# A decoder step's mixer: its steps given other places beside the paged past

## The chip, the cores and the metric

One core of a Trainium2 chip runs the whole program. Its engines are TensorE (PE, matmul; PEld is its weight load), VectorE (DVE), ScalarE (ACT), GpSimd (POOL, which here mainly issues the gathers of cache pages) and SyncE (SP, which issues the other transfers). Each engine works through its own instructions in the order in which the program was built, and waits for others by semaphores. The metric is the device time of one execution in microseconds, as the median of several runs; lower is better.

## The reference

Two layers of a hybrid decoder, for 592 tokens: a prompt of 16 + 512 and 8 samples of 8 new tokens each. A layer is a half-step feed-forward block, a mixer and another half-step feed-forward block. Cut to the mixer:

```python
z, xbc, dt_raw, q, k, v = split(h @ w_in)
xbc_c = silu(causal_conv(xbc))                   # xs, B, C
y = ssd_scan(xs, softplus(dt_raw + dt_bias), -exp(A_log), B, C, h0) + D_skip * xs
y_ssd = group_rms_norm(y * silu(z)) * ssd_norm
q, k = rms_norm(q) * q_norm, rms_norm(k) * k_norm          # each head
# prompt: stick-breaking attention over itself, blocks of 128 queries
# samples: the same over 2048 cached keys in pages of 128, and their own new keys
#   z = q.k / 8 + bias;  w = sigmoid(z) * prod of (1 - sigmoid) over the later keys
o = w @ v
y_sb = rms_norm(o) * sb_out_norm
out = concat(y_ssd, y_sb) @ w_out
```

All is float32. A gemm keeps that precision by splitting each operand into a high and a low part and adding three products (high x high, low x high, high x low).

## The kernel before

Activations lie transposed: 8 tiles of 128 features x 592 tokens. `gemm` runs over pairs of output tiles of 128 columns; for each 512 rows of weights it loads `raw` (SP), splits it into `whi` (ACT, L595) and `wlo` (DVE, L596), and issues matmuls of 128x128 weights on 296 tokens into two PSUM banks (`g`, L605). When an output tile is complete, `done` takes it out of PSUM.

The mixer first runs the gemms of the queries (`queries`) and values (`values`), then traces the paged past (`past`), and after that the other steps in the order of the list `ORDER`. The past runs over 8 samples in 4 steps each: two page gathers of keys and two of values (POOL, L1508 and L1569), four transposes `kt` on DVE (L1519), a group of 32x128 matmuls `sc` for scores and `po` for weighing the values of the sample six steps behind, and per sample sigmoids, products `st` on DVE and transposes into weights. 34 such steps and four more for the last values.

The other steps: `dts` (time steps), `conv` (gemm of six tiles, convolution), `k` (gemm of the keys), `z` (gemm of the gates, `gate_in`, tiles `zi`, `zsg`), `scan` (six chunks of the state recurrence; the last, for the samples, also loads and stores their states), `kfin` (the keys' norm, `head_norm`: squares `hsq`, sums `ss`, a reciprocal root `ry`, spread over the partitions as `hb`, product onto `k`), `vout` (loads the values back as `vk`), `Pa-b` (prompt attention, blocks a to b-1 of 12, `pair_blocks`: scores `z`, sigmoids `be` and `st`, transposes `zt`, output `zo`), `mix` (gates and norm of the scan's output), `newk` (the samples' own keys), `tail` (the last 16 prompt queries), `kout` (stores keys), `xload` (loads the residual back). The output gemm `wo` comes last; its first half, over the scan's output, is tied behind the past's last scores, weights and weighing.

The order on each engine isn't written out. The program is built with a planner (`schedule_with_timeline_sim=True`) which, whenever an engine is free, takes the ready instruction with the lowest number. An instruction's number is its place in the traced program, unless `ahead` lowers it: `high_priority(now - d)` sets the number to d places after the past's first instruction. `PRI` gives d for a whole step, or, as `gemm:x`, for the weight splits and the `done` of a gemm; `UNIT` gives it for a single output tile of a gemm, a chunk of the scan or a prompt block. Where both are silent, a step keeps the number of its place, behind the whole past. The matmuls of a gemm always keep it.

Tiles come from pools with few slots: `g` has 3 PSUM banks (in the mixer behind the past `NARROW`, so all gemms, `kfin`, prompt blocks and `kout` draw on these three), `pm` 2, the others one each for the past; in SBUF `tmp` has 6 slots, `xh` 16 (the 16 tiles of the split hidden state until the last gemm of `w_in` has read them, then `vk`, `be`, `st` and the split operands of `wo`), and `kn` 6 for pages of keys and values alike.

```python
d = PRI.get(what) if what else PRI.get("gemm:" + self.gn, PRI["gemm"])
return nullcontext() if d is None else self.tc.high_priority(max(0, now - d))
```

Of the kernel before, what the change touches and what calls it, by code (L numbers as in the profile page):

```python
# [84 lines left out]
def pack(d):  # L85
# [6 lines left out]

ORDER = "dts conv k z scan kfin vout P0-8 P8-10 P10-12 mix newk tail kout xload".split()
PRI = {"gemm": 508, "scan": 0, "kfin": 1140, "newk": 2458, "dts": 0, "gemm:k": 0, "gemm:conv": 199, "gemm:wo": 693, "tail": 799, "gemm:z": 1391}
UNIT = {
    "conv0": 296, "conv2": 988, "conv3": 1825, "conv5": 1898, "k1": 434, "k2": 1127, "k3": 936, "prompt0": 1013,
    "prompt1": 2161, "prompt11": 2222, "prompt2": 2280, "prompt3": 1185, "prompt4": 2319, "prompt5": 1429,
    "prompt6": 106, "prompt7": 1403,  # L100
    "scan0": 467, "scan2": 75,
    "scan3": 879, "scan5": 123, "wo0": 0, "wo1": 2358, "wo2": 1775, "wo3": 86, "wo4": 1087, "wo5": 1599, "wo6": 529,
    "wo7": 1477, "z1": 0, "z2": 970, "z3": 1087,
}


class Kern:
# [515 lines left out]
    def ahead(self, what=None, unit=None):  # L623
# [3 lines left out]
        now = self.tc.cur_priority - self.p0  # L627
        u = UNIT.get(f"{what or self.gn}{unit}") if unit is not None else None
        if u is not None:
            return self.tc.high_priority(now - u)  # L630
        if what and unit is not None:
            return nullcontext()
        d = PRI.get(what) if what else PRI.get("gemm:" + self.gn, PRI["gemm"])
        return nullcontext() if d is None else self.tc.high_priority(max(0, now - d))
# [78 lines left out]
    def mixer(self, l):  # L713
# [36 lines left out]
        def xload():  # L750
            self.xtiles()
            for k in range(KD):
# [6 lines left out]
                 "tail": lambda: self.prompt_tail(q, S["k"]), "newk": lambda: self.new_keys(q, S["k"])}  # L759
        for st in ORDER:  # L760
            self.gn = st
# [885 lines left out]
```

## Time and profile before

| | us |
|---|---|
| median of 3 runs | 2688.8 |
| lowest, highest | 2679.9, 2701.8 |
| profiled execution | 2681.4 |
| its span, first to last instruction | 2679.6 |

The first mixer's work beside the past lies at about 527 to 920 us of the span, the second's at about 1864 to 2245; the feed-forward blocks around them keep PE busy without a break. In the span's strip of 40 slices these are slices 9 to 13 and 28 to 33. The profile gives busy time per engine for any stretch; on PE the matmuls are pipelined, so that busy time says when PE had work, not how well it was used. The granted clock is the share of full speed that PE was given. Rows by tile give the first and last start of each kind of instruction, and so when a step ran.

DVE is the second engine by load. The transfers of the past come at their highest rate in the later half of its time (slices 11 and 31 of the DMA strip):

```profile
DVE  6434346397886743444554343465878957444444
DMA  3232234467973222222222323244678731222222
GB/s 113 80 115 82 85 113 131 127 214 264 336 241 129 70 81 79 79 79 79 79 79 79 97 85 100 78 151 164 223 253 300 249 128 56 88 86 79 85 89 76
```

### The profile page before, as it was taken

What the parts mean: (1) busy time and instruction counts of PE and PEld (TensorE: products, weight loads), DVE (VectorE), ACT (ScalarE), POOL (GpSimd) and SP (SyncE); (2) the same over time, 40 slices, a digit from 0 to 9 for tenths busy, and PEclk for the clock granted to TensorE, in tenths of its full rate; (3) what the DMA queues carried; (4) which work ended last, traced back from release to release, by engine and by line L of the source; (5) the groups of instructions that cost most, each with busy time, mean ns of one, the idle gap of its engine ahead of it and who ended that gap; (6) DMA issues with size and microseconds to landing.
All of it is one profiled execution on the core that took longest, in us unless ns stands there. A gap on an engine that the chain in (4) does not pass through costs nothing.

```text
span 2679.6 us, 51326 instructions
## 1 busy us (share of the span) xinstructions
PE 2600.5 (97%) x21547; PEld 2466.6 (92%) x21547; DVE 1505.1 (56%) x3005; ACT 978.9 (37%) x1771; POOL 304.7 (11%) x288
## 2 busy tenths in 40 slices
PE   8999999999889999999999999999998899999999
PEld 7999999898657999999999999998886579999998
DVE  6434346397886743444554343465878957444444
ACT  3222224256564432222332222233566634223222
POOL 1000000034532100000000000001345411000000
PEclk9999999999989999999999999999998999999999
DMA  3232234467973222222222323244678731222222
GB/s 113 80 115 82 85 113 131 127 214 264 336 241 129 70 81 79 79 79 79 79 79 79 97 85 100 78 151 164 223 253 300 249 128 56 88 86 79 85 89 76
DMA packets 245112, 343.28 MB, mean 128 GB/s; under 512 B 32809, under 2 KB 196721, under 8 KB 244881
## 3 DMA queue, kind: packets, MB, share of 16 engines
q1 hardware_dynamic: 208016, 205.77, 24.7%
q0 software_dynamic: 36864, 134.23, 14.5%
q8 instruction: 169, 2.77, 0.4%
q14 instruction: 63, 0.51, 0.1%
HBM read 320.29 MB, written 19.66 MB: 127 GB/s over the span
## 4 chain that ended last, share of the span: by engine, by line
PE 84%; DVE 7%; issue 3%; ACT 3%; DMA 2%; POOL 1%; SPq 0%; DVEq 0%; POOLq 0%; ACTq 0%
PE g L605 72%; PE v L926 2%; DVE kt L1519 2%; PE po L211 1%; PE sc L211 1%; DMA v<-in_cache_v,vi 1%; DVE st L1298 1%; PE pw L476 1%; DMA kn<-in_cache_k,ki 1%; DVE pst L1298 1%; POOL v L1569 0%; PE z L208 0%; PE z L211 0%; DVE xl L447 0%; DVE wlo L596 0%
## 5 line engine op out<-in xcount | busy, mean ns | idle before, releaser
L605 PE MATMUL g<-xl,whi 128*128 128x296 f32 (+1 forms) x3392 | 1014.6, 299 | 2.7 <-DVE xl L447 2.7
L605 PE MATMUL g<-xh,wlo 128*128 128x296 f32 (+1 forms) x3392 | 1012.9, 299 | 2.0 <-DVE wlo L596 2.0
L605 PE MATMUL g<-xh,whi 128*128 128x296 f32 (+1 forms) x3392 | 1011.1, 299 | 1.5 <-DVE gs L231 1.2
L595 ACT ACTIVATE whi<-raw 128x512 fp32r<-128x512 f32 (+1 forms) x664 | 412.6, 622 | 1323.6 <-PE g L605 1240.5
L596 DVE TENSOR_TENSOR wlo<-raw,whi 128x512 fp32r<-128x512 f32 (+1 forms) x664 | 450.3, 678 | 582.8 <-ACT whi L595 529.7
L605 PEld LDWEIGHTS g<-xl,whi 128*128 128x128 f32 x3392 | 638.6, 188 | 5.6 <-DVE xl L447 3.6
L605 PEld LDWEIGHTS g<-xh,wlo 128*128 128x128 f32 x3392 | 638.7, 188 | 4.3 <-DVE wlo L596 2.5
L605 PEld LDWEIGHTS g<-xh,whi 128*128 128x128 f32 x3392 | 638.7, 188 | 4.0 <-DVE gs L231 1.4
L605 PE MATMUL g<-hl,whi 128*128 128x296 f32 (+1 forms) x1408 | 417.8, 297 | 0.0
L605 PE MATMUL g<-hh,wlo 128*128 128x296 f32 (+1 forms) x1408 | 417.6, 298 | 0.0
L605 PE MATMUL g<-hh,whi 128*128 128x296 f32 (+1 forms) x1408 | 416.7, 298 | 0.0
L1508 POOL DMA_INDIRECT kn<-in_cache_k,ki x128 | 128.3, 1003 | 1657.9 <-PE g L605 934.8
L605 PEld LDWEIGHTS g<-hl,whi 128*128 128x128 f32 x1408 | 265.2, 188 | 0.0
L605 PEld LDWEIGHTS g<-hh,wlo 128*128 128x128 f32 x1408 | 264.3, 188 | 0.0
L605 PEld LDWEIGHTS g<-hh,whi 128*128 128x128 f32 x1408 | 263.9, 188 | 0.0
L1519 DVE STREAM_TRANSPOSE kt<-kn 128x512 f32<-128x512 f32 x256 | 162.9, 681 | 27.7 <-PE sc L211 14.5
L704 DVE SCALAR_TENSOR_TENSOR x<-g,x 128x296 f32<-128x296 f32 (+1 forms) x192 | 88.1, 463 | 119.1 <-PE g L605 118.5
L1569 POOL DMA_INDIRECT v<-in_cache_v,vi x128 | 143.3, 1119 | 100.0 <-DVE kt L1519 36.1
L231 DVE TENSOR_TENSOR us<-g,R 128x296 f32<-128x296 f32 (+1 forms) x176 | 81.5, 464 | 129.1 <-PE g L605 129.0
L231 DVE TENSOR_TENSOR gs<-g,R 128x296 f32<-128x296 f32 (+1 forms) x176 | 80.6, 463 | 126.2 <-PE g L605 121.3
L691 ACT ACTIVATE hh<-us 128x592 fp32r<-128x592 f32 (+1 forms) x88 | 61.2, 696 | 64.3 <-DVE us L689 64.3
L605 PE MATMUL g<-mh,whi 128*128 128x296 f32 (+1 forms) x256 | 77.7, 312 | 2.4 <-ACT mh L1277 1.3
(372 smaller groups left out, 2838.8 us busy)
## 6 DMA issues: line engine op xcount, KB each, us to landing
raw<-in_ffn_w_gu SPq DMA_DIRECT2D x176, 512.0 KB
raw<-in_ffn_w_down SPq DMA_DIRECT2D x80, 512.0 KB
raw<-in_w_in SPq DMA_DIRECT2D x44, 512.0 KB
raw<-in_w_out SPq DMA_DIRECT2D x16, 512.0 KB
spill<-x SPq DMA_DIRECT2D x16, 296.0 KB
x<-spill SPq DMA_DIRECT2D x16, 296.0 KB
raw<-in_ffn_w_down SPq DMA_DIRECT2D x16, 256.0 KB
xt<-in_x_prompt SPq DMA_DIRECT2D x8, 256.0 KB
```

Of the source, the lines that this page charges most:

```text
L211: i = self.nc.tensor.matmul(*a, **k).ins
L231: self.nc.vector.tensor_tensor(tv[0:P, h, :], ps[h][0:P, 0:self.n], rv[0:P, h, :], ALU.mult)
L595: nc.scalar.activation(hi[:, 0:nk], s, AF.Copy)
L596: nc.vector.tensor_tensor(lo[:, 0:nk], s, hi[:, 0:nk].bitcast(F32), ALU.subtract)
L605: mm = nc.tensor.matmul(ps[h][:, 0:self.n], w[:, k, :], self.hv(x)[:, h, :], start=(first and k == 0 and i == 0), stop=(last and k == nk - ...
L691: nc.scalar.activation(hh[:, a:b], u[:, a:b], AF.Copy)
L704: nc.vector.scalar_tensor_tensor(v, p, 0.5, v, ALU.mult, ALU.add)
L926: nc.tensor.matmul(ps[c], x[:, t0:t0 + 128], w.rearrange("p x c -> p (x c)"), start=(k == 0 and i == 0), stop=(k == 7 and i == 2))
L1298: self.nc.vector.tensor_tensor_scan(sv, sv, self.zero[0:rows].to_broadcast([rows, b - a - 1]), 1.0, ALU.mult, ALU.add)
L1508: self.nc.gpsimd.indirect_dma_start(kn, None, self.kflat, bass.IndirectOffsetOnAxis(ap=self.kidx[self.l][:, s, 2 * i + u:2 * i + u + 1], a ...
L1519: self.nc.vector.transpose(kt[:, 2 * u:2 * u + 2].rearrange("p t h i -> p t (h i)"), kns[u][:, :, 256 * quad:256 * quad + 256])
L1569: self.nc.gpsimd.indirect_dma_start(v.rearrange("p k c -> p (k c)"), None, self.vflat, bass.IndirectOffsetOnAxis(ap=self.vidx[self.l][:, s ...
```

## The change

Only the three tables of places differ; no instruction is added or removed by them.

```diff
-ORDER = "dts conv k z scan kfin vout P0-8 P8-10 P10-12 mix newk tail kout xload".split()
-PRI = {"gemm": 508, "scan": 0, "kfin": 1140, "newk": 2458, "dts": 0, "gemm:k": 0, "gemm:conv": 199, "gemm:wo": 693, "tail": 799, "gemm:z": 1391}
-UNIT = {
-    "conv0": 296, "conv2": 988, "conv3": 1825, "conv5": 1898, "k1": 434, "k2": 1127, "k3": 936, "prompt0": 1013,
-    "prompt1": 2161, "prompt11": 2222, "prompt2": 2280, "prompt3": 1185, "prompt4": 2319, "prompt5": 1429,
-    "prompt6": 106, "prompt7": 1403,
-    "scan0": 467, "scan2": 75,
-    "scan3": 879, "scan5": 123, "wo0": 0, "wo1": 2358, "wo2": 1775, "wo3": 86, "wo4": 1087, "wo5": 1599, "wo6": 529,
-    "wo7": 1477, "z1": 0, "z2": 970, "z3": 1087,
-}
+ORDER = "dts conv k kfin z scan vout P0-12 mix newk tail kout xload".split()
+PRI = {"gemm": 508, "scan": 0, "kfin": 60, "newk": 560, "dts": 0, "gemm:k": 60, "gemm:conv": 0, "gemm:wo": 693, "tail": 600, "gemm:z": 120}
+UNIT = {f"prompt{i}": 300 + 25 * i for i in range(12)}
```

In the order of the trace, `kfin` stands between the gemms of keys and gates instead of behind gates and scan, and the twelve prompt blocks are traced in one run instead of three (a run finishes a block's output after the next block's scores are traced; at the end of a run it is finished at once). In the numbers, `kfin` goes from 1140 to 60, `newk` from 2458 to 560, `tail` from 799 to 600, the gates' splits and evictions from 1391 (single tiles 0, 970, 1087) to 120, the convolution's from 199 (single tiles up to 1898) to 0, the keys' from 0 (single tiles up to 1127) to 60. All chunks of the scan are at 0. Every prompt block has a number, 300 to 575 in steps of 25. The output gemm's eight tiles, which had numbers from 0 to 2358, are all at 693.

## The prediction

> **What bounds the kernel now.** I read the page first, for the engines' shares and the strip of 40 slices, then busy time in stretches of the first mixer and of the second, then the instructions on single tiles, to see which step ends each stretch.
>
> ```profile
> span 2679.6 us, 51326 instructions
> PE 2600.5 (97%) x21547; PEld 2466.6 (92%) x21547; DVE 1505.1 (56%) x3005; ACT 978.9 (37%) x1771; POOL 304.7 (11%) x288
> PE   8999999999889999999999999999998899999999
> PEclk9999999999989999999999999999998999999999
> ```
>
> PE works for 97% of the span, and every dip in its strip lies in the two mixers. Nothing in the change adds or removes arithmetic, so the time can change only by what PE idles there, and by the clock it gets. The two mixers, cut where the work changes (columns: length, busy us of PE, PEld, DVE, ACT, POOL, granted clock, DMA share, GB/s):
>
> ```profile
> 527.00:630.00 103.00, 101.04 (x1101) 91.73 (x1100) 85.64 (x203) 60.55 (x125) 34.71 (x32) 1.00 0.69 224
> 630.00:693.00 63.00, 60.83 (x750) 52.80 (x752) 53.35 (x118) 36.15 (x73) 30.58 (x30) 1.00 0.90 318
> 693.00:736.00 43.00, 35.71 (x497) 24.76 (x486) 37.01 (x89) 23.78 (x58) 23.23 (x24) 0.96 0.93 331
> 736.00:846.00 110.00, 93.26 (x1003) 67.34 (x1007) 91.25 (x213) 66.42 (x140) 36.13 (x33) 0.89 0.63 213
> 846.00:920.00 74.00, 72.17 (x581) 69.92 (x574) 51.08 (x92) 30.47 (x54) 10.13 (x6) 0.98 0.19 58
> 2036.00:2070.00 34.00, 28.65 (x416) 20.41 (x412) 27.74 (x59) 19.90 (x40) 18.07 (x16) 0.85 0.77 262
> 2070.00:2160.00 90.00, 74.19 (x854) 52.48 (x847) 80.80 (x183) 55.29 (x118) 40.77 (x36) 0.96 0.77 261
> ```
>
> While the gemms of conv, keys and gates last (527 to 693), PE is 97 to 98% busy: the gemms carry the largest numbers and fill every hole that the paged past leaves. From 693 no gemm is left until 846, and PE falls to 83% and 85%. Idle there: 43 - 35.71 = 7.3 and 110 - 93.26 = 16.7 us; in the second mixer 34 - 28.65 = 5.4 and 90 - 74.19 = 15.8. That is 45.2 us, 1.7% of the span, and it is nearly all that a new order can win. DVE is close behind: 91.25 of 110 and 80.80 of 90, 83% and 90%.
>
> What fills 693 to 736 is the norm of the keys (rows of the tile view: duration minimum/median/maximum, first and last start):
>
> ```profile
> L231 DVE TENSOR_TENSOR k<-g,R x8: 444/458/467, 593.4 to 628.0; 128x296 f32<-128x296 f32 x8
> L231 DVE TENSOR_TENSOR zi<-g,R x8: 444/454/466, 640.3 to 691.0; 128x296 f32<-128x296 f32 x8
> L879 ACT ACTIVATE hsq<-k x4: 678/680/682, 693.5 to 695.3; 128x592 f32<-128x592 f32 x4
> L890 DVE SCALAR_TENSOR_TENSOR k<-k,par,hb x8: 284/508/747, 721.1 to 735.7; 128x512 f32<-128x512 f32 x4, 128x80 f32<-128x80 f32 x4
> L947 SPq DMA_DIRECT2D vk<-vd x6: 338/536/600, 679.9 to 682.7; - x6
> L208 PE MATMUL z<-k,q x24: 376/587/792, 733.3 to 828.6; 64*128 64x512 f32 x8, 64*128 64x384 f32 x8, 64*128 64x256 f32 x8
> ```
>
> The raw keys are there at 628. Their squares wait until 693.5, although ACT is busy for only 36.15 of 63 us: `hsq` takes a slot of the pool `tmp` behind the gates' `zi`, whose last eviction is at 691. I read from this that slots go out in program order, so the order in `ORDER` decides. The norm then takes 42 us, and the first prompt scores follow at 733.3, 105 us after the keys. The values for them were asked for at 680.
>
> **The change, step by step.** Positions: `ahead` puts a step beside the past's own count, where only the first matmul of a `together` group counts. By my count one of the 8 sequences has 76 places (9 in each of its 4 steps for issues, transposes and the group, 8 sigmoids, 4 copies, 24 for the weights, 4 for the sum), so the past has 608 places and a step some 18. Before, all prompt numbers but one lie beyond 608 or are missing: blocks run where the past leaves room. After, they lie at 300 to 575, one per 25 / 18 = 1.4 steps.
>
> (a) `kfin` moves from behind the gates to behind the keys, and from 1140 to 60. It issues no DMA. On PE, ACT and DVE it now goes ahead of most of the past, and from the pools for PSUM banks (`g`, three) and `tmp` it takes its slots ahead of the gates' gemm. So the hole at 693 goes, 7.3 + 5.4 = 12.7 us. In its place comes a hole between keys and gates: `kfin` takes seven banks in turn, and the gates' gemm cannot have a pair until the last few are out. That gemm is what covers PE there; only past and scan remain. With the same chain at the same idle share this hole costs all 12.7 again. It should be shorter: the 13 operations of the reciprocal root run as follows,
>
> ```profile
> L523 DVE TENSOR_SCALAR ry<-rv x4: 141/172/180, 710.4 to 924.7; 128x5 int32<-128x5 int32 x2, 128x40 int32<-128x40 int32 x1, 128x10 int32<-128x10 int32 x1
> L529 DVE TENSOR_TENSOR rlo<-ry,rhi x5: 159/169/194, 501.8 to 928.6; 128x40 fp32r<-128x40 f32 x2, 128x5 fp32r<-128x5 f32 x2, 128x10 fp32r<-128x10 f32 x1
> ```
>
> each about 0.17 us long, 13 x 0.17 = 2.2 us of work, and yet from the keys' `ry` at 710.4 to the first `k` product at 721.1 there pass 11 us, since transposes of 0.68 us stand in front. With the front place I take half the chain and half the cost: 6.3 us. Net -6.3, ends -12.7 and 0.
>
> (b) The prompt blocks wait for `kfin` and for the slots of pool `xh` that the hidden state holds until the gates' gemm has read it. With 42 us of norm gone from behind that gemm and some 21 put in front of it, they begin about 20 us sooner. The past pays: blocks now stand ahead of its later steps on PE, ACT and DVE. How far it has come by then in the run before (DVE busy on the pages' transposes, 128 in all with 4 ahead of the first row):
>
> ```profile
> 520.00:693.00 173.00, 47.81 (x76) 1.00 0.76 258
> 693.00:736.00 43.00, 15.53 (x24) 0.96 0.93 331
> 736.00:846.00 110.00, 15.23 (x24) 0.89 0.63 213
> ```
>
> At 736 only 24 of 128 transposes are left, 6 steps; they and the value steps behind them share 110 us with 12 blocks. After, more steps share the stage with the same blocks. DVE is 83 and 90% busy here, so mixing them does not shrink the sum of DVE's work; I take 0 for the stage itself. Ends: half its idle goes, -16.3, or the past is late (the first rival).
>
> (c) `tail` from 799 to 600 and `newk` from 2458 to 560 come before the past's end. In the run before, `tail` stands in the output gemm, which is 97.5% busy in the first mixer (tile `z` and the scan operand `st`, first and second mixer):
>
> ```profile
> 846.00:920.00 74.00, 8.59 (x123) 6.63 (x114) 0.45 (x2) 4.67 (x12) 0.98 0.19 58
> 846.00:920.00 74.00, 3.91 (x4) 1.93 (x4) 0.98 0.19 58
> 2160.00:2245.00 85.00, 9.19 (x124) 6.87 (x122) 0.45 (x2) 4.67 (x12) 0.94 0.18 59
> 2160.00:2245.00 85.00, 4.48 (x6) 1.93 (x4) 0.94 0.18 59
> ```
>
> 8.59 + 9.19 = 17.8 us of PE move into a stage that idles; but 3.91 + 4.48 = 8.4 us of DVE go with them into a stage where DVE is 87% busy on average, which lengthens it by 8.4 / 0.87 = 9.7. Net -8.1, ends -17.8 and 0.
>
> (d) The whole scan at 0 (two chunks had 467 and 879), the conv evictions at 0, gates at 120, output gemm at 693. Until 693 PE is full, so moving DVE work about within this stretch frees nothing: 0. Its cover is the gemm filler; if DVE, 53.35 of 63 us busy, let it starve, a tenth of 63 us in each mixer would be 12.6 us. SP's and POOL's queues keep their transfers; only their order changes, and the past's pages queue behind evictions for at most a few operations.
>
> Sum: -6.3 + 0 - 8.1 + 0 = -14.4. The profiled execution took 2681.4 us (its span 2679.6 and 1.8 around it), so 2667.0. It is 7.5 us below the median of the three runs, 2688.8; against that median the forecast is 2674.4, say 2675, 0.5% less. A measurement of this kernel can tell about 1%, 27 us, from no change.
>
> **The rivals.** *The past is left over (slower).* Scan, norm, gates and most blocks now go first; what they take is taken from the past, which then ends alone, with no gemm to fill it, since the output gemm is tied behind the past's last scores. Price from 693 to 736: 24 transposes are 6 steps in 43 us at a DMA share of 0.93, 7.2 us a step, the best pace seen. PE's part of it in that stretch:
>
> ```profile
> 693.00:736.00 43.00, 5.47 (x160) 4.06 (x160) 15.53 (x24) 0.96 0.93 331
> 693.00:736.00 43.00, 7.44 (x99) 3.44 (x88) 0.59 (x2) 0.00 (x0) 0.96 0.93 331
> 693.00:736.00 43.00, 2.37 (x11) 1.54 (x11) 0.68 (x4) 1.20 (x2) 0.96 0.93 331
> ```
>
> (scores, weighing, weights): 15.3 / 6 = 2.5 us a step, so a step alone idles PE for 4.7 us. Five steps too many in each mixer cost 47 us: 2675 + 47 = 2722; six 56, 2731. It decides from (14.4 + 27) / (2 x 4.7) = 4.4 steps. For it: at 736 the past now has a lead of 104 transposes of 128, and it loses that lead. Against it: one block per 1.4 steps, the last at step 575 / 18 = 32 of 34, so by the numbers both end together.
>
> *The stage fills (faster).* If the hole in front of the gates closes (-12.7) and past and blocks together keep PE at the 96.6% of the stretch from 630 to 693, idle falls from 32.5 to 0.034 x 200 = 6.8, another -25.7: 2688.8 - 38.4 = 2650. Against it: that stretch had a gemm to fill it, this one has none, and DVE at 90% is in the way.
>
> *The clock comes back (faster).* In the four weak stretches PE's granted clock is 0.96, 0.89, 0.85 and 0.96; with PE full it is 1.00. Lost: 0.04 x 43 + 0.11 x 110 + 0.15 x 34 + 0.04 x 90 = 22.5 us. If denser work brought all of it back, 2675 - 22.5 = 2652. Against it: the stretch keeps most of its holes, and much of the small work waits on other engines, not on PE's clock. The Trainium skill, "TensorE: Matmul & The Clock Gate", Part 1, says that the array runs at half rate after an idle window of about 3.4 us and at full rate after a busy one; the rows above agree in direction, 1.00 with PE at 97% and 0.85 at 84%, and by that rule alone the sum would be the 2652 just worked out.
>
> *It does nothing.* If the gates' gemm loses in front what the blocks gain behind it, blocks start again at 733; with `tail` alone, -8.1, 2681.
>
> **How the numbers follow.** The forecast 0.45 and the change that does nothing 0.09 stay within 1% (2662 to 2716); the filled stage 0.14 and the clock 0.06 make 0.20 faster; the late past 0.26 is slower. The likeliest has its own range of 2662 to 2689. Range for all: from 2642, below both faster cases by what (c) has at its far end, to 2736, the late past with six steps in each mixer and a little of (d). Outside I leave half of the extremes, some 0.15 to 0.2.
>
> **What would show it.** Right: `hsq` follows the last raw key at once, and the norm takes some 20 us; the first prompt scores stand 15 to 25 us sooner after the mixer's start; `tail` lies before the past's last weighing; PE's idle in the four weak stretches, with the new holes between keys and gates, falls from 45 to about 31 us. (a) is wrong if the gates' gemm starts more than 35 us after the last key, (b) if the last block ends more than five steps before the past, (c) if the output gemm is no shorter. The whole is wrong if PE's idle in the mixers grows.

## The result: 0.5% slower

| | before | after |
|---|---|---|
| median, us | 2688.4 | 2700.4 |
| lowest, highest | 2679.9, 2701.8 | 2694.1, 2709.5 |
| profiled execution | 2681.4 | 2709.5 |

The ratio after to before is 1.0051, with a 95% interval of 1.0041 to 1.0062. The forecast was 0.5% less. Each median is over 20 executions. The two profiled ones stand at opposite ends of their runs, 7 us below the one median and 9 above the other, so a comparison of their stages shows the loss more than twice as large as the 12 us it is.

The page of the changed kernel (first the span and PE's total, then strips of 40 slices: busy share of PE and of DVE in tenths, the granted clock, the share of the DMA engines):

```profile
span 2707.5 us, 51317 instructions
PE 2619.9 (97%) x21547; PEld 2480.7 (92%) x21547; DVE 1504.2 (56%) x3005; ACT 984.5 (36%) x1775; POOL 313.3 (12%) x288
PE   8999999998978999999999999999989899999999
DVE  5444445397787744443554344464977967434444
PEclk9999999999988999999999999999989999999999
DMA  3232234467875122222222322244667941222222
```

PE's idle time is 2707.5 - 2619.9 = 87.6 us, where it was 79.1. In the two mixers alone it is 68.9 us (527 to 941 and 1889 to 2271), where it was 61.7 (527 to 920 and 1864 to 2245): the whole is worse, by the prediction's own test. The other 19.4 us are busy time, and PE has the same 21547 matmuls: its clock is lower, 0.980 over the run where it was 0.987. That is the lowest clock of the changed kernel's 20 executions, whose median is 0.984, so part of this busy time belongs to the execution that was profiled and not to the change.

The evictions of the output gemm's second half (`ot`) end each mixer. First and second mixer before, then after:

```profile
L231 DVE TENSOR_TENSOR ot<-g,R x16: 448/452/467, 893.8 to 916.9; 128x296 f32<-128x296 f32 x16
L231 DVE TENSOR_TENSOR ot<-g,R x16: 440/444/457, 2227.1 to 2251.2; 128x288 f32<-128x288 f32 x16
```

```profile
L224 DVE TENSOR_TENSOR ot<-g,R x16: 448/453/467, 916.7 to 941.6; 128x296 f32<-128x296 f32 x16
L224 DVE TENSOR_TENSOR ot<-g,R x16: 440/444/458, 2253.6 to 2277.7; 128x288 f32<-128x288 f32 x16
```

The first ends 24.7 us later; from there to the end of the second it is 1336.1 us for 1334.3. In these two executions nearly the whole difference arises in the first mixer. It is shown here, cut where the work now changes (columns as before):

```profile
527.00:637.00 110.00, 106.68 (x1135) 94.67 (x1132) 87.68 (x210) 61.33 (x125) 34.30 (x32) 1.00 0.64 214
637.00:682.00 45.00, 37.07 (x518) 28.02 (x519) 38.41 (x95) 21.97 (x53) 26.21 (x26) 0.96 0.89 310
682.00:736.00 54.00, 51.87 (x545) 45.89 (x545) 39.25 (x89) 34.16 (x65) 18.54 (x19) 0.97 0.80 276
736.00:866.00 130.00, 105.25 (x1173) 73.75 (x1171) 102.12 (x222) 73.03 (x155) 49.96 (x44) 0.87 0.67 230
866.00:941.00 75.00, 73.47 (x574) 70.80 (x573) 49.92 (x99) 28.82 (x52) 10.13 (x5) 0.95 0.17 52
```

The hole of the norm is there again, 45 - 37.07 = 7.9 us between 637 and 682, where 7.3 us lay between 693 and 736. New is that the stretch without a gemm lasts 130 us where it lasted 110, and idles 24.75 where it idled 16.7. The tile rows show why the steps didn't move as forecast (first and last start):

```profile
L224 DVE TENSOR_TENSOR k<-g,R x8: 446/456/459, 593.6 to 636.7; 128x296 f32<-128x296 f32 x8
L872 ACT ACTIVATE hsq<-k x4: 693/697/697, 595.2 to 637.1; 128x592 f32<-128x592 f32 x4
L883 DVE SCALAR_TENSOR_TENSOR k<-k,par,hb x8: 252/498/739, 670.9 to 678.7; 128x512 f32<-128x512 f32 x4, 128x80 f32<-128x80 f32 x4
L224 DVE TENSOR_TENSOR zi<-g,R x8: 442/462/467, 689.5 to 734.8; 128x296 f32<-128x296 f32 x8
L201 PE MATMUL z<-k,q x24: 376/588/1006, 735.7 to 844.3; 64*128 64x512 f32 x8, 64*128 64x384 f32 x8, 64*128 64x256 f32 x8
L1400 DVE COPY tail<-z x2: 217/222/227, 882.5 to 899.1; 64x64 f32<-64x64 f32 x2
L516 DVE TENSOR_SCALAR ry<-rv x1: 162/162/162, 649.1 to 649.1; 128x40 int32<-128x40 int32 x1
L522 DVE TENSOR_TENSOR rlo<-ry,rhi x1: 200/200/200, 663.7 to 663.7; 128x40 fp32r<-128x40 f32 x1
```

The squares follow the last raw key at once (637.1 after 636.7), as forecast. But the norm takes 42 us again, from 637 to 679: in the front place its root alone is spread from 649.1 to 663.7 among the operations of scan and past. The gates' gemm starts at 677.1, 40 us after the last key, and its first eviction comes 53 us after it (689.5); the prediction had named 35 us as the sign that (a) is wrong. The first prompt scores come at 735.7, where they came at 733.3, and `tail` still lies in the output gemm, which is no shorter (75 us for 74).

What is late in this trace is the past. The DVE rows of its page transposes from 500 to 780 us, and the evictions of its outputs, before and then after:

```profile
500.00:780.00 280.00, 73.52 (x116) 0.96 0.75 255
L1594 DVE COPY oP<-po x2: 169/180/192, 822.9 to 840.2; 128x32 f32<-128x32 f32 x2
```

```profile
500.00:780.00 280.00, 66.89 (x104) 0.97 0.70 237
L1587 DVE COPY oP<-po x3: 174/181/192, 818.4 to 866.5; 128x32 f32<-128x32 f32 x3
```

(Counted over this one stretch; sums of short stretches, as some expectations below have them, come out one or two higher, since an instruction on a border counts in both.) Twelve transposes fewer are three steps, and the last sample's output comes 26 us later, 866.5 for 840.2. Where the past loses its time is seen on POOL, which asks for the pages: in the timeline, the idle time before a gather, with what ended it, stands at the end of the row. Before, then after:

```profile
688.20 0.93 POOL L1508 DMA_INDIRECT kn<-in_cache_k,ki  x1 [6.14 <-PE po L211]
```

```profile
698.38 0.94 POOL L1501 DMA_INDIRECT kn<-in_cache_k,ki  x1 [13.56 <-PE po L204]
738.58 1.16 POOL L1501 DMA_INDIRECT kn<-in_cache_k,ki  x1 [14.83 <-PE po L204]
```

Gathers come in fours, one step's worth, and every fourth step, at the end of a sample, they stop until `po` has weighed values and freed their slots. It can't weigh before the sample's weights exist. Added up from 610 us on, the stops over 4 us are 60.9 us before and 75.9 after. The chain that makes the weights, around 680 us, before and then after (carry, copy of its transposed products, weights):

```profile
L1543 DVE COPY car<-pw x1: 136/136/136, 672.9 to 672.9; 2x32 f32<-2x32 f32 x1
L1548 DVE COPY cq<-pw x1: 138/138/138, 675.3 to 675.3; 128x2 f32<-128x2 f32 x1
L1558 ACT ACTIVATE wt<-pw x2: 597/597/597, 678.9 to 682.6; 128x512 f32<-128x512 f32 x2
```

```profile
L1536 DVE COPY car<-pw x1: 171/171/171, 677.9 to 677.9; 2x32 f32<-2x32 f32 x1
L1541 DVE COPY cq<-pw x1: 151/151/151, 685.1 to 685.1; 128x2 f32<-128x2 f32 x1
L1551 ACT ACTIVATE wt<-pw x1: 601/601/601, 688.8 to 688.8; 128x512 f32<-128x512 f32 x1
```

(The query ended at 690 us, so the second weights of the changed kernel are not in its row.) From the start of the carry to that of its copy there are three small operations on DVE and a transpose on PE; they took 2.4 us and now take 7.2, though each on DVE is shorter than 0.2 us. They stand in the queues among the work that now goes in front. That is 4.8 us more, while the stop grew by 7.4.

### The profile page after: what moved, and what is told of

Same layout as the page of the kernel before. It is cut to its first block, busy times and chain, and to the rows that moved or that the text cites. A ratio compares the mean times of both kernels' runs of the same rounds, so it can differ in the third digit from the quotient of the medians.

```text
span 2707.5 us, 51317 instructions
## 1 busy us (share of the span) xinstructions
PE 2619.9 (97%) x21547; PEld 2480.7 (92%) x21547; DVE 1504.2 (56%) x3005; ACT 984.5 (36%) x1775; POOL 313.3 (12%) x288
## 4 chain that ended last, share of the span: by engine, by line
PE 83%; DVE 8%; DMA 3%; ACT 3%; issue 2%; POOL 0%; SPq 0%; DVEq 0%; ACTq 0%; POOLq 0%
PE g L598 73%; PE v L919 2%; DVE kt L1512 2%; DMA v<-in_cache_v,vi 2%; DMA kn<-in_cache_k,ki 1%; PE po L204 1%; DVE st L1291 1%; PE sc L204 1%; PE pw L469 1%; PE z L201 1%; DVE pst L1291 1%; PE z L204 0%; DVE be L1336 0%; PE po L201 0%; PE sc L201 0%
```

## The experiments

Three theories were set against each other. A: the hole in front of the gates is the loss, because the norm holds the three banks of `g`. D: the end of the scan's last chunk sets the mixer's end, through the gates' norm and the first half of the output gemm. L, later W: what is put in front makes the past late, at the weights' chain. Ratios are against the kernel before, run beside each; its own medians ranged from 2685 to 2713 us between groups of runs, so times of different groups are not compared. Places in a trace are, below, and they scatter too. One kernel, the blocks alone, was traced in two groups; its past ended at 844.7 us in one and at 855.1 in the other, with 115 and 108 transposes by 780 us. A difference of some 10 us or 7 transposes between traces of different groups therefore shows nothing by itself.

**The parts alone.** The norm's move:

```diff
-ORDER = "dts conv k z scan kfin vout P0-8 P8-10 P10-12 mix newk tail kout xload".split()
+ORDER = "dts conv k kfin z scan vout P0-8 P8-10 P10-12 mix newk tail kout xload".split()
-"kfin": 1140
+"kfin": 60
```

> The kernel before, with only the keys' norm moved in front of the gates and to 60; blocks and all other numbers as before. Theory A: this alone brings the loss, about 2700 (2695 to 2706). Theory B: the move alone gains, 2670 to 2685, since blocks stay behind the past. Theory C: 2688, give or take 5.

2705.0 us, 1.0067 (1.0044 to 1.0091): the norm's move alone brings a loss as large as the whole change. The blocks' numbers and their one run alone:

```diff
-P0-8 P8-10 P10-12
+P0-12
+UNIT.update({f"prompt{i}": 300 + 25 * i for i in range(12)})   # in place of the eight old prompt numbers
```

> The kernel before, with only the prompt blocks traced in one run and at 300 to 575; the keys' norm stays behind the gates. Theory A: no loss, 2684 to 2692. Theory B: the loss, 2697 or more, with page transposes later and the past's last weighing behind the last block. Theory C: 2684 to 2692.

2687.0 us, 0.9983 (0.9968 to 0.9998). The blocks cost nothing. All the other numbers alone (`ORDER`, `kfin` and the prompt numbers as before):

```diff
+PRI = {"gemm": 508, "scan": 0, "kfin": 1140, "newk": 560, "dts": 0, "gemm:k": 60, "gemm:conv": 0, "gemm:wo": 693, "tail": 600, "gemm:z": 120}
+UNIT = the prompt numbers of before, nothing else
```

> The kernel before with only the other numbers of the change: convolution's evictions 0, keys' 60, gates' 120, output gemm 693 for all tiles, whole scan 0, newk 560, tail 600. The keys' norm stays behind the gates at 1140, the prompt blocks keep their old numbers and runs. Theory A (only the norm's place costs): nothing changes, 2688 +- 3 us. Theory C (these numbers bring a share of the loss): the kernel with the norm put back (2695.3) is 8.3 us above the one with the blocks alone (2687.0), and differs from it by just these numbers; if that is theirs whatever the blocks do, 2688.4 + 8.3 = 2697 us. In both cases the norm stands near 693 to 736 us in the first mixer. Theory D (what sets a mixer's end is the last chunk of the scan, through the gates and the first half of the output gemm): the time follows the end of that chunk in the first mixer, 783.8 us before and 797.9 us with the norm put back; 2697 us goes with an end near 798 us, 2688 us with one near 784 us.

2699.6 us, 1.0050 (1.0033 to 1.0066), with the norm at its old place behind the gates. So the loss is there without the hole in front of the gates, and A can't be all of it. Two parts each bring the whole loss, and together they bring it once. The changed kernel with only the norm put back:

```diff
-k kfin z scan
+k z kfin scan
```

> The changed kernel with only the keys' norm traced behind the gates again (its number stays 60). Theory A, banks in program order: the norm in front holds the three g banks for its whole chain and so keeps the gates' gemm out; put back, the hole between keys and gates closes, the gates' gemm starts within 5 us of the last key and the time falls from 2700 to about 2688 (2682 to 2694). Theory B, late past: blocks with numbers inside the past cost the 12 us; then this stays at 2697 to 2704. Theory C, the other numbers (convolution, scan, single output tiles): also 2697 to 2704.

2695.3 us, 1.0022 (1.0008 to 1.0036): the norm's place is worth some 0.3 points there.

**The banks.** The changed kernel with the norm on the two banks of `pm` in place of `g`:

```diff
-"kfin": lambda: self.head_norm(S["k"], "k_norm", ("g",))
+"kfin": lambda: self.head_norm(S["k"], "k_norm", ("pm",))
```

> The changed kernel, but the keys' norm takes its banks from the pool pm (two banks) and leaves the three g banks to the gemms. Theory A: the gates' gemm starts within 5 us of the last key and runs under the norm, the first prompt scores stand 15 to 25 us sooner, and the time falls to 2675 to 2690. Theory B: blocks that start sooner make the past still later, 2700 or more. Theory C: within 6 us of 2700. Against all: the scan's chunks share pm with the norm and may stand still for its 42 us.

2758.9 us, 1.0269 (1.0245 to 1.0294). The stages 617 to 665 and 740 to 920 us, the first prompt scores, and the scan's outputs:

```profile
617.00:665.00 48.00, 48.00 (x607) 41.41 (x607) 35.40 (x82) 17.69 (x42) 20.89 (x21) 1.00 0.84 290
740.00:920.00 180.00, 149.96 (x1417) 116.68 (x1417) 113.66 (x264) 80.58 (x169) 48.92 (x43) 0.78 0.52 171
L201 PE MATMUL z<-k,q x24: 376/534/693, 664.8 to 785.7; 64*128 64x512 f32 x8, 64*128 64x384 f32 x8, 64*128 64x256 f32 x8
L1167 DVE SCALAR_TENSOR_TENSOR xc<-xc,dcol,yt x20: 279/343/351, 702.0 to 851.4; 128x128 f32<-128x128 f32 x16, 128x64 f32<-128x64 f32 x4
```

The banks did make the hole: with others, the gates' gemm runs under the norm with PE 100% busy, and the blocks start 70 us sooner. And yet this is far slower. The scan, which needs `pm`, ends at 851.4 where it ended at 808.1, and from 740 on PE has no gemm left and idles 30 of 180 us at a clock of 0.78. With the scan's first two chunks traced ahead of the norm:

```diff
-k kfin z scan
+k scan0-2 kfin z scan2-6
```

> The changed kernel with the norm on the two banks of pm as in the run that took 2758.9 us, but with the scan's first two chunks traced ahead of the norm, so that they don't wait for it. The gates' gemm again starts within 15 us of the last key, and the blocks near 665 to 690 us. Theory D (those 2758.9 us came from the scan, whose first chunk ended 72 us late and whose last ended 43 us later than in the changed kernel): two chunks gain their time back, so the last one ends near 815 to 830 us in place of 851, and the time lies half way, 2715 to 2735 us. Rival (the loss came from the gemm that is used up early, so that nothing fills PE behind it): the gates' gemm ends as early as there, and the time stays at 2745 to 2765 us.

2732.2 us, 1.0172 (1.0146 to 1.0197): within the range that D gave, though the last chunk still ended at 856, not sooner than 851. So the gain doesn't come from that end, and D's reason isn't borne out by it. The norm cut in two, on the kernel with the blocks alone: squares, sums and root on `pm` in front of the gates, spread and products on `g` behind them. Both halves have 60 in place of 1140, and the scan's first two chunks are traced in front of the gates.

```diff
-k z scan kfin vout
+k scan0-2 kroot z scan2-6 kprod vout
```

> The kernel with the blocks alone, with the norm cut in two: squares, sums, transposes and root stand in front of the gates' gemm, behind the scan's first two chunks, and draw on the two banks of pm; spread and products stay behind the gates and draw on g. Theory A (the hole came from the three banks of g that the norm held): the gates' gemm starts within some 15 us of the last raw key, as before (12 us), what is left of the norm behind the gates takes 10 to 15 us in place of 42, and the first prompt scores come 20 to 30 us sooner than 733 us in the first mixer. If the blocks' start is what counts, half of the hole of 12.7 us goes and more follows from the earlier blocks: 2675 to 2682 us. Theory D (the end of the scan's last chunk sets the mixer's end): the scan waits for pm for some 15 us; the last chunk ends at 785 to 800 us, and the time is 2685 to 2697 us, however early the blocks start.

2692.2 us, 1.0026 (1.0008 to 1.0043). The first scores came at 702.5, 31 us sooner than before, and the time rose. An early start of the blocks is worth nothing here, though this run also moved scan and norm.

**The scan's end.** The changed kernel with the states of samples 4 to 7 loaded into slots of `tmp`:

```diff
-H0 = self.ssd("h0", [128, 2, 2, 2, 64], "hx")
+H0 = self.ssd("h0", [128, 2, 2, 2, 64], "hx") if s2 < 2 else self.tmp("h0", [128, 2, 2, 2, 64])
```

> The changed kernel with one thing more: in the scan's last chunk the states of samples 4 to 7 are loaded into two slots of tmp in place of the two slots that samples 0 to 3 hold until their new states are stored. Nothing else is moved; the norm keeps its place and its chain. Theory D (the end of the scan's last chunk sets the mixer's end): that chunk, which runs from 717 to 808 us in the first mixer and from 2075 to 2152 us in the second, gets 10 to 25 us shorter, its loads are asked for earlier, and the time falls by about as much as the end moves, for two mixers: from 2700 to 2680 to 2692 us. Rival (the norm's hole alone costs, or the past's end): the chunk ends sooner, the time stays at 2700 +- 3 us.

2705.8 us, 1.0072 (1.0050 to 1.0094). In the second mixer the scan's last output comes at 2138.4 for 2151.8 in the changed kernel, and the past's last one hardly moves:

```profile
L1167 DVE SCALAR_TENSOR_TENSOR xc<-xc,dcol,yt x8: 278/310/346, 2067.7 to 2138.4; 128x128 f32<-128x128 f32 x4, 128x64 f32<-128x64 f32 x4
L1587 DVE COPY oP<-po x2: 183/183/183, 2188.1 to 2214.7; 128x32 f32<-128x32 f32 x2
```

(2214.7 for 2213.1.) But the first mixer ended 5.6 us sooner here (936.0 for 941.6). Counted from that end, the scan comes 8 us sooner, the past 7 us later, and the second mixer ends 6 us later. A scan that ends sooner gives nothing, so D's forecast of 2680 to 2692 us fails. The first mixer speaks against L as the whole cause: there the past ended at 848.2, where it ended at 866.5 in the changed kernel, and the kernel is no faster:

```profile
L1587 DVE COPY oP<-po x3: 181/191/191, 802.6 to 848.2; 128x32 f32<-128x32 f32 x3
```

**Which numbers.** The kernel before with scan and gates alone at the new numbers, then each by itself (the edit in short):

```diff
-"gemm:z": 1391     and tiles z1: 0, z2: 970, z3: 1087
+"gemm:z": 120
-scan0: 467, scan2: 75, scan3: 879, scan5: 123
+all chunks at "scan": 0
```

> The kernel before, with two of the other numbers alone: every chunk of the scan at 0 (two had 467 and 879, two 75 and 123) and the gates' splits and evictions at 120 (before 1391, single tiles 0, 970, 1087). Theory L (the mixer ends some 75 us behind the past's last sample, and whatever is put in front of the past makes it late): scan and gates now go in front in the stretch from 640 to 720 us, where the run with all the other numbers did 9 of the past's page transposes from 690 to 720 us in place of 16. So most of the 0.5% of that run comes back: 2695 to 2700 us, past's end 10 to 20 us later than 842 us. Rival (output gemm's, tail's and newk's numbers bring it): 2688 +- 3 us, past's end near 842 us.

> The kernel before with one number changed: the gates' splits and evictions at 120 in place of 1391 (tiles 0, 970, 1087). Together with the scan at 0 this brought 0.84%. Theory W: the gates' products and sigmoids on DVE and ACT stand in front of the weights' chain at about 680 us, where the gathers stopped for 19.4 us in that run and for 6.1 us before; the stop is over 12 us here too, and at least half of the loss shows: 2696 to 2704 us. Rival (the scan's numbers bring it): the stop near 682 us is 6 to 9 us, and the time is 2688 +- 3 us.

> The kernel before with the scan's numbers alone changed: all six chunks at 0 (chunk 0 had 467, chunk 3 had 879, chunks 2 and 5 had 75 and 123). The gates' number alone left the time as it was (ratio 0.9998), both together brought 0.84%. Theory W (what is put in front of the past makes it late): chunk 3 at 0 stands in front of the weights' chain of some sample, the page transposes done by 780 us fall below 112 (before 117), the past's last output comes after 848 us, and the time is 0.4 to 0.9% above before. Rival (only both together do it): within 0.2% of before.

Both: 1.0084 (1.0051 to 1.0116), more than all the other numbers together, past's last output at 857.2. Gates alone: 0.9998 (0.9978 to 1.0017). Scan alone: 1.0028 (1.0012 to 1.0043), which is below the 0.4 to 0.9% expected, 104 transposes by 780 us and the past's last output at 863.9, where the blocks alone, in the same group, had 855.1. With the gates' number alone the stop near 682 us, expected at over 12 us, was 6.5; with the scan's numbers alone it was 17.1:

```profile
692.88 0.94 POOL L1508 DMA_INDIRECT kn<-in_cache_k,ki  x1 [6.47 <-PE po L211]
705.47 0.94 POOL L1507 DMA_INDIRECT kn<-in_cache_k,ki  x1 [17.09 <-PE po L210]
```

So it is the scan in front that holds the weights' chain. The gates add to the loss only beside it; why they do is not shown.

**The past.** Five slots for pages in place of six, on the kernel with the blocks alone:

> The kernel with the blocks alone (2687.0 us), with five slots in place of six for pages of keys and values, all numbers kept. This slows the past and nothing else that stands in the mixer's order. Theory L (the past's end sets the mixer's end): the past's last output comes later than 847 us in the first mixer, and the mixer's last product stays 74 to 80 us behind it; if the past, bound by its slots, loses a tenth of its 320 us, that is up to 30 us a mixer, 2700 to 2745 us. Theory D (the end of the scan's last chunk sets it): the scan, gates and norm don't use these slots; the last chunk ends near 785 us as before or sooner, and the time stays within 2682 to 2694 us.

2717.4 us, 1.0110 (1.0087 to 1.0132). 6 us of the 30 lie ahead of the first mixer's keys (603.7 for 597.5); the input's load uses these slots too. Counted from the keys, the first mixer's past ends only 2 us later. In the second mixer, counted from the end of the first, the past's last output comes 15 us later than with six slots, the scan's end 2 us, and the mixer's end 18: it follows the past, not the scan. (The products of the gates' norm come 16 us later too.) The whole past put ahead by 150 places in the changed kernel (150 added to every other number that lies beside it):

> The changed kernel with the past moved ahead by 150 places, some 8 of its 34 steps: scan, norm, gates, keys, convolution, newk, tail and prompt blocks all get 150 more, so that their order among themselves is kept, the norm in front of the gates too. Theory L: the past is less late, with more than the 87 transposes that the changed kernel had done by 720 us; its last output comes at 850 to 860 us in place of 866.9, and the time is 2685 to 2695 us. Theory D: the scan now stands behind the past's first steps, its last chunk ends later than 808 us, and the time is 2705 to 2725 us. Theory A (the hole in front of the gates alone): the hole is kept, the time stays at 2700 +- 4 us.

2701.5 us, 1.0055 (1.0037 to 1.0074). L's forecast missed: 104 transposes by 780 us, no more than in the changed kernel, though the past's last output came at 856.6. The stop of the gathers that ends near 700 us was 12.1 us here, for 13.6: moving all of the past hardly moved its chain. So the next one moved only the chain, in the changed kernel:

```diff
+with self.tc.high_priority(700):
     self.sigmoids(...)
+with self.tc.high_priority(700):
     wts[s] = self.past_weights(s, be, st)
```

> The changed kernel with the past's weights first: the sigmoids and the chain that makes a sample's weights (scan, totals, carry, products, transposes, copy) get numbers 700 places lower, ahead of norm, scan, gates and prompt blocks; everything else keeps its number, the norm in front of the gates too. Theory W (the loss comes through the past: at the end of each sample its pages stay in the six slots until the next weights are there, and what the change puts in front lengthens that chain): in the first mixer the stops of the page gathers over 4 us, 75.9 us in all from 610 us on in the changed kernel and 60.9 before, fall by 10 us or more; more than 106 of the 128 page transposes are done by 780 us; the past's last output comes before 858 us in place of 866.5, and the time is 2680 to 2693 us. Theory A (the hole in front of the gates itself is the loss): the hole of some 8 us stays, and so does the time, 2700 +- 4 us. Theory D (the end of the scan's last chunk): the scan gets later, not sooner, than 808 us, and the time is 2700 to 2712 us.

Ratio 1.0020 (1.0004 to 1.0036), where the changed kernel had 1.0051. The gathers, the past's outputs and the products of the gates' norm (`ml`):

```profile
695.13 0.94 POOL L1503 DMA_INDIRECT kn<-in_cache_k,ki  x1 [7.36 <-PE po L204]
727.67 0.94 POOL L1503 DMA_INDIRECT kn<-in_cache_k,ki  x1 [6.02 <-PE po L204]
...
500.00:780.00 280.00, 69.88 (x110) 0.95 0.72 242
...
L1589 DVE COPY oP<-po x2: 166/168/170, 825.4 to 843.2; 128x32 f32<-128x32 f32 x2
...
L431 DVE TENSOR_TENSOR ml<-xc,mh x4: 741/766/776, 858.0 to 861.7; 128x592 fp32r<-128x592 f32 x4
```

The two stops fall from 13.56 and 14.83 us to 7.36 and 6.02, and all stops over 4 us from 75.9 to 60.0; the past ends at 843.2 for 866.5, as early as before. In the chain of the sample of the first stop, carry to copy still takes 8.1 us, in the next 2.4 for 5.8. The norm still stands in front of the gates, and PE still idles there, 63 - 53.11 = 9.9 us from 630 to 693. By the ratios three fifths of the loss are gone, (0.51 - 0.20) / 0.51, though the hole is not. The two ratios come from different groups, with the kernel before at 2688 and 2712 us, but their intervals don't meet. What is left: now the gates' norm is late, at 861.7 for 837.7 before (844.0 with the gates' number alone, in the group of this run), and the output gemm has to wait for that. In this trace the first mixer is in fact no shorter, its last `ot` at 943.5 for 941.6, so where the time came back isn't shown.

The same lift where nothing holds the chain, on the blocks alone, then on the split norm, and beside that the blocks alone once more:

> The kernel with the blocks alone (2687.0 us) with the same lift of the past's sigmoids and weights. There the stops of the gathers over 4 us were 49.1 us in the first mixer. Theory W: what is left of them gets shorter still where the chain waited for other work; half of the 10 to 19 us stops at 568, 612 and 794 us goes in the best case, and the time falls to 2675 to 2685 us. Rival (in this kernel the chain already went first, its stops are the chain's own length): 2687 +- 3 us.

> The kernel with the norm cut in two, whose blocks began at 702.5 us and whose past ended last (850 us, the products of the gates' norm at 834 us), with the past's weights first as well. Join theory (the mixer ends with the later of two chains, the past, and scan, gates, tail): the past comes sooner than 845 us, the other chain is some us later than 834 us, they meet near 840 us, and the time falls from 0.26% above before to between 0.3% below and 0.1% above. Rival (what one chain gains the other loses in full): the products of the gates' norm come after 850 us, and the time stays 0.1 to 0.4% above before.

> The blocks alone once more, beside the other two on one chip: the first time it was at 0.9983 of before. If that gain is real, 0.997 to 0.999 again; if it is scatter between chips, 1.000 +- 0.001. The join theory says nothing but that it isn't slower, since both chains end within 3 us of each other there as before.

1.0013 (0.9993 to 1.0034), 1.0075 (1.0049 to 1.0101) and 0.9999 (0.9980 to 1.0019). The lift is no gain by itself. On the split norm the join theory's forecast missed: the gates' norm came at 863.0 and the past's last output at 861.5, both later. The blocks alone are as fast as the kernel before; no version here is faster than these two.

One number separates most of these runs: the stop of the gathers that ends near 700 us in the first mixer. It is 5.8 to 6.5 us in the five traces of kernels without a clear loss (the kernel before, the blocks alone twice, the gates' number alone, the blocks with the weights first). It is 10.5 to 19.4 us in all twelve slower kernels that leave six slots and the weights' numbers as they were. The past's end doesn't separate them: 840 to 855 us in the five, 848 to 869 in the twelve. And the length of this stop doesn't give the size of the loss: 16.3 us goes with 1.0022 (norm behind the gates), 12.4 with 1.0269 (norm on `pm`). With the weights first it is 7.4 us in the changed kernel (1.0020). It is 7.3 on the split norm, which is 0.75% slower, so a short stop doesn't suffice.

**The tail.** The changed kernel with `tail` traced ahead of `mix`:

```diff
-mix newk tail
+tail mix newk
```

> The changed kernel with tail traced ahead of mix; all numbers kept, tail at 600. If tail stayed behind mix because its banks and slots are handed out in the order of the trace, its outputs now come ahead of the products of the gates' norm, at some 840 to 865 us in the first mixer in place of 882 to 899, beside the past's last steps. Theory of the prediction's step (c): PE's 8.6 us a mixer leave the output gemm and fill holes, DVE pays, net some -4 us a mixer: 2690 to 2696 us. Theory L: tail goes in front of the past's last steps and of mix on DVE, so the past's end is no sooner and mix is later: 2700 to 2708 us.

2743.3 us, 1.0213 (1.0190 to 1.0236), far outside both forecasts:

```profile
L1400 DVE COPY tail<-z x2: 218/223/228, 847.0 to 864.7; 64x64 f32<-64x64 f32 x2
L431 DVE TENSOR_TENSOR ml<-xc,mh x4: 768/772/776, 877.2 to 881.7; 128x592 fp32r<-128x592 f32 x4
L1418 DVE TENSOR_TENSOR zs<-zn,b x2: 417/417/417, 883.3 to 883.7; 64x256 f32<-64x256 f32 x2
```

`tail` moved by 35 us, so the order of the trace had held it. But `mix` and `newk` now come behind it, 28 and 37 us later than in the changed kernel (853.9, 846.4), and both are needed for the output.

## Where the prediction was right and wrong

The direction was wrong: where the sum has -6.3 us for the norm in front and 0 for the other numbers, each alone costs time, 18 and 13 us. The step that failed is to price both by PE's holes and PE's filler alone, and to leave out what stands in front of the past's small chain of weights. By its steps:

- *(a), the norm in front, "I take half the chain and half the cost", -6.3 us: failed.* In the first mixer the chain stayed at 42 us and the hole at 7.9. That alone would make the step zero, the end of its range. Measured alone it costs 0.67%, some 18 us, beyond that end: the bounds were taken from the hole, and not from what the step does to the past's small chains. There the stop near 700 us is 14.4 us for 6.1.
- *(b), the blocks, 0 for the stage: right on the price* (0.9983 and 0.9999 alone), wrong that they begin 20 us sooner (735.7). In the split norm, which moved scan and norm as well, 31 us sooner won nothing.
- *(c), tail and newk ahead of the past's end, -8.1 us: failed.* Number 600 doesn't move a step whose banks and slots are handed out behind `mix`. The prediction had read that rule from `hsq` and didn't apply it here. Done by the order of the trace, the move costs 2.1 - 0.5 = 1.6 points. (Two slips in the sum change nothing: the 4.48 us of DVE hold some 0.6 us of two products of a prompt block, and the average share of DVE is 86%.)
- *(d), the other numbers, 0, "moving DVE work about within this stretch frees nothing": failed.* Alone they cost 0.50%, 13 us; the price named for the lost cover was 12.6. That the two agree is luck, as the place was another: PE was 94% busy from 632 to 693 us there (57.24 of 61), for 97%, so little of it is a starved gemm. The scan's numbers alone cost 0.28%, with the stop near 700 us at 17.1 us. The rest of the 0.50% was not taken apart.
- *The rival of the past left over:* the nearest to what the runs show, by the stops, by five slots and by the chain put first, but not in its reason: the past is held up at its weights' chain. Its size was too large: at 780 us the past is 3 steps behind, not 5 or 6, and its 4.7 us a step, for two mixers, would be 28 us; the median rose by 12. The page gathers could have shown it in the run before, had their stops been read: 60.9 us in one mixer while the past has 230 us left.
- *It does nothing:* right for (a) and (b) in the trace, blocks at 735.7 for 733.3.
- *The clock:* it went the other way, 0.87 from 736 to 866 us. The Trainium skill, "TensorE: Matmul & The Clock Gate", Part 1, which says that the array falls to half rate after an idle window, agrees in direction here too, with 24.75 us idle in that stretch.

Not settled: why the norm in front alone costs 0.67% and the other numbers alone 0.50%, but the whole change only 0.51%. Nor is it shown how a late past becomes time in each mixer. In the second mixer of the changed kernel the past's last output comes 17 us later than before, counted from the end of the first, and the mixer ends only 2 us later; with the states loaded ahead the first mixer's past ends as early as in kernels without a loss, and the kernel is 0.72% slower. So the hold-up of the weights' chain goes with the loss in twelve kernels, and easing it took back part of the loss, but that it is the whole cause is not shown. That the two chains, past on one side, scan and gates' norm on the other, take time from each other is seen in one kernel only, that with the weights first.

## What to carry to other kernels

Where a ring of few buffers feeds a long chain, look for the small operations that free its slots, and ask what a new order puts in front of them; here that told more than the largest hole of the busiest engine. A lower number may not move a step whose banks or slots are handed out in the order of the trace. And when a stretch may be set by several chains that meet at one join, don't count an earlier start of one step as a gain before you know which chain arrives last.

## What the hardware showed beside that

- A page of 512 KB, gathered by POOL, landed 6.7 us (values; median, least 5.6) or 7.4 us (keys; least 5.7) after its issue between 690 and 780 us of the changed kernel, with a DMA share of 0.80 from 682 to 736. The Trainium skill, "DMA: Bandwidth & Descriptors", section "Anatomy of one DMA — SWDGE (gpsimd) path", gives 2.0 us and bytes by 436e3; by this estimate a page takes 3.2 us. The measurement is twice that and decides.
- Granted clock: 0.78 over the 180 us in which PE was 83% busy with small groups (the norm on `pm`), against 1.00 in the same run from 617 to 665, at 100%. The busy share alone doesn't give the clock: it was 0.96 in the changed kernel from 637 to 682, at 82%.
- The kernel before had medians from 2685 to 2713 us in different groups of runs, 1%, as much as most effects here; only ratios inside a group could be read.
